# First projections of a diffusion step: order of the first loads, and modulation sums in column groups

## The chip, the cores and the metric

The program runs on one core of one Trainium2 chip. The metric is the time of one execution in device microseconds (us). TensorE is called PE here, VectorE DVE, ScalarE ACT, GpSimd POOL, and SyncE, which issues the transfers, SP.

## The reference

One layer of a backbone is computed for 128 context tokens and 2048 latent tokens of width 1024, all in float32. What matters here is the start of it:

```python
m = silu(cond) @ w_mod + b_mod          # cond: c_ctx and c; w_mod: 1024 x 6144
sh1, sc1, ga1, sh2, sc2, ga2 = split(m, 6)
h = rmsnorm(x, norm_mix) * (1 + sc1) + sh1
proj = h @ w_in                          # 1024 x 3088
q, k, v = split(silu(centred_conv(proj[:, :1536], conv_w)), 3)
```

So `h` needs the first 2048 columns of `m`, that is 8 MB of `w_mod`, and the first projections need `h` and the columns of `w_in` that make k. A gated DeltaNet scan, spatial gating, the output projection and the MLP follow, and the outputs are both token streams and the scan's final states.

## The kernel before

The kernel is written with a tile framework. A planner orders the instructions of every engine by a simulated timeline in which instructions that stand earlier in the program go first where several are ready; it also assigns buffers and waits. The order on an engine, SP's queue included, is fixed when the program is built; an engine whose next instruction waits does nothing else.

The 17 tiles of 128 tokens are projected in six blocks (`BLOCKS`), of which block 0 holds the context tile and two latent tiles. In a block, twelve feature tiles of 128 columns are projected: (1, h) are k, (0, h) q and (2, h) v. Every projection is float32-like: inputs and weights are split in a high and a low part (`split_w`, L200 on ACT and L201 on DVE), and three products (L226 to L228) per 128 rows of weights are accumulated. A feature tile thus has 8 x 3 products in one accumulator (`pj`, three buffers; `pt`, three buffers, for transposes and for the feature tile (1, 2) of block 0). Then it is evicted by the convolution (`convolve`: L553 on ACT, L556 on DVE).

Block 0's inputs need the modulation. `mod_load` loads half of one vector's weights, eight tiles of 128 x 512 (`raw`, L189), and `mod_sum` sums them in eight float32 products with `scond` (two columns, one per condition) as the weight (L337). ACT copies the row out (L339), `mod_out` turns it into columns with four transposes (L346) and adds the bias on DVE (L349, L353). `m0` and `r0` are the first half of the shift `b1`, `m1` and `r1` that of the scale `a1`, `m2` and `m3` the second halves. The first halves serve columns 0 to 3 of the inputs, the second ones columns 4 to 7.

`norm_rows` normalises a row tile (L320, L322). `column(k)` of block 0 transposes 128 columns of three row tiles (L499), applies scale and shift on ACT (L501), splits on DVE (L504, L505) into `kH` and `kL`, sets edge and halo columns on POOL (L491, L492; L494, L495), and stores both to DRAM (L519, four stores per column). `first_half` prepares the halo columns (L424 to L428). The next block's rows come with `load_x` (L447), whose squares ACT sums (L452); they use the three buffers of `xs0`.

Order of the loads on SP before: `m0`, the small vectors, `m1`, `m2`, the ten halo rows `xh`, three row tiles `xs0`, `m3`, four tiles of `W1[1]`, then the rest of `W1[1]` and `W1[0]` among column stores. `WARM` is 8: that many products of ones (L296) open the program on PE.

Of the kernel before, what the change touches and what calls it, by code (L numbers as in the profile page):

```python
# [8 lines left out]
F32 = mybir.dt.float32  # L9
# [8 lines left out]
P = 128  # L18
# [45 lines left out]
def hybrid_step(  # L64
# [11 lines left out]
    def xrow(t):  # L76
        return x_prompt[0] if t == 0 else x_sample[0, (t - 1) * P : t * P, :]
# [98 lines left out]
    def pm1():  # L176
        return pmp.tile([P, 512], F32, tag="pm", name="pm", bufs=2)
# [102 lines left out]
    with ExitStack() as ph:  # L280
# [52 lines left out]
        def mod_sum(raws, psum):  # L333

            pm = psum()
            for k in range(KT):
                T.matmul(pm[0:2, :], scond[:, k, :], raws[k], start=k == 0, stop=k == KT - 1)  # L337
            row = pf.tile([2, 512], F32, tag="first", name="first", bufs=2)
            A.copy(row, pm[0:2, :])  # L339
            return row  # L340

        def mod_out(row, half, dst, bias, scaled):

            pc = pm1()
            for i in range(4):
                T.transpose(pc[:, 2 * i : 2 * i + 2], row[:, i * P : (i + 1) * P], ident[0:2, 0:2])  # L346
            ks = slice(half * 4, half * 4 + 4)
# [8 lines left out]
        def split_mod_steps(jc):  # L356
# [23 lines left out]
            return [lambda k=k: f(k) for k in range(KT)]  # L380

        m0 = mod_load(0, 0)
# [12 lines left out]
        for m in range(5):  # L395
            load(out=xh[2 * m : 2 * m + 2, :], in_=x_sample[0, 255 + 384 * m : 257 + 384 * m, :])
        r2 = mod_sum(m2, pj)
# [7 lines left out]
        V.tensor_copy(hal, ps[:, 0:80].rearrange("p (k j) -> p k j", k=KT))  # L405
        xs0 = []
        for t in BLOCKS[0]:
            x = p1.tile([P, D], F32, tag="x", name="x", bufs=3)
            load(out=x, in_=xrow(t))
            xs0.append(x)  # L410
        for x in xs0:
            norm_rows(x)

        def load_w1(gi, ks):
            return [w1_raw(gi, k) for k in ks]

        def w1_raw(gi, k):
            return raw_w(w_in[0, k * P : (k + 1) * P, gi * 512 : (gi + 1) * 512])

# [10 lines left out]
        def prep_block(bi):  # L430
# [49 lines left out]
            if bi == 0:  # L480
                zc, hc = [0, 129, 130], [(387, 1)]
            elif bi == 5:
                zc, hc = [n + 1], [(0, 8)]
            else:
                hc = [(0, 2 * bi - 2), (n + 1, 2 * bi + 1)]
            def column(k):
                full = p1.tile([P, 384], F32, tag="full", name="full", bufs=2)
                kH = p1.tile([P, 388], F32R, tag="h", name="kH", bufs=24)
                kL = p1.tile([P, 388], F32R, tag="h", name="kL", bufs=24)
                for col in zc:  # L490
                    G.tensor_copy(kH[:, col : col + 1], zcol[:, 0:1])  # L491
                    G.tensor_copy(kL[:, col : col + 1], zcol[:, 0:1])  # L492
                for col, j in hc:
                    G.tensor_copy(kH[:, col : col + 1], f32(halH)[:, k, j : j + 1])  # L494
                    G.tensor_copy(kL[:, col : col + 1], f32(halL)[:, k, j : j + 1])  # L495
                if bi == 0:
# [32 lines left out]
        def feature_tile(blk, bi, gi, h):  # L529
# [229 lines left out]
        wr = load_w1(0, range(KT))  # L759
        us = [feature_tile(blk, 0, 1, h) for h in range(3)]  # L760
        for k in range(4):
            cols[k]()
            for u in us:
                u["main"][k]()
        mod_out(r3, 1, a1, vec[:, 8:16], True)
        W1[1] += [split_w(r) for r in wk]
        first_half(1)
# [1191 lines left out]
```

## Time and profile before

| | us |
|---|---|
| three runs | 2596.32, 2599.12, 2601.89 |
| median | 2599.12 |
| the profiled execution, its own time | 2598.87 |
| its span in the profile | 2596.8 |

In the profile, busy time is by engine, PE for products and PEld for the loading of their weights. L337 is line 337 of the kernel; an entry such as `pm<-raw,scond` names the tile written and the tiles read. "SPq" is SP's queue issuing a transfer. "idle before" gives the time that the engine stood idle ahead of an instruction, and who ended it. A float32 product is two records on PE. Records of products overlap, so the cost of a product is read from start to start.

### The profile page before, as it was taken

The numbers are of one execution on the slowest core, as the hardware profiler recorded it, in microseconds if no ns is written. First come the engines' busy times: TensorE is split into PE (matmuls) and PEld (weight loads), VectorE is DVE, ScalarE is ACT, GpSimd is POOL, SyncE is SP. The second block draws the span as 40 slices with busy tenths as digits, with TensorE's granted clock in tenths as the row PEclk, the third lists the DMA queues.
The fourth block names the chain that finished last, engine by engine and source line by source line (L and its number), as shares of the span: only waits on it lengthen the run. The fifth ranks groups of instructions, "written<-read, shape, count | busy, mean of one in ns | idle before, by whom it ended". The sixth has DMA issues, their size and how long they took to land.

```text
span 2596.8 us, 44648 instructions
## 1 busy us (share of the span) xinstructions
PE 2553.3 (98%) x15508; PEld 2156.5 (83%) x15508; DVE 1801.0 (69%) x3733; ACT 1220.9 (47%) x3048; POOL 228.8 (9%) x448
## 2 busy tenths in 40 slices
PE   9999999899999999999999999999999999999998
PEld 5999999688888787778888888888888888888887
DVE  5867756766667878886678876666665557784874
ACT  4755555554555667764355643332342432243441
POOL 3112212111111111210000000000000000000000
PEclk9999999899999999999999999999999999999999
DMA  8977738645445657885768789444479979786773
GB/s 288 304 212 214 209 109 266 201 148 154 154 144 166 208 173 248 275 275 181 279 204 256 224 283 307 114 118 118 123 234 370 334 268 321 270 256 213 236 247 106
DMA packets 494695, 571.88 MB, mean 220 GB/s; under 512 B 35124, under 2 KB 297564, under 8 KB 490886
## 3 DMA queue, kind: packets, MB, share of 16 engines
q1 hardware_dynamic: 494470, 569.04, 68.2%
q8 instruction: 122, 2.00, 0.3%
q14 instruction: 103, 0.84, 0.1%
HBM read 389.23 MB, written 179.67 MB: 219 GB/s over the span
## 4 chain that ended last, share of the span: by engine, by line
PE 87%; DVE 5%; DMA 4%; ACT 1%; issue 1%; POOL 0%; SPq 0%; DVEq 0%; POOLq 0%; ACTq 0%
PE f L226 16%; PE f L228 16%; PE f L227 16%; PE pj L226 7%; PE pj L228 7%; PE pj L227 7%; PE pd L995 5%; PE f L1599 2%; PE pm L226 1%; PE pm L227 1%; PE pm L228 1%; PE pt L610 1%; PE pt L569 1%; DMA QK<-qk_d 1%; PE pd L1076 1%
## 5 line engine op out<-in xcount | busy, mean ns | idle before, releaser
L226 PE MATMUL f<-hop,zH 128*128 128x512 f32 x960 | 373.4, 389 | 1.2 <-ACT zH L1485 1.2
L228 PE MATMUL f<-hop,zL 128*128 128x512 f32 x960 | 373.4, 389 | 0.4 <-DVE zL L1479 0.4
L227 PE MATMUL f<-hop,zH 128*128 128x512 f32 x960 | 373.3, 389 | 0.0
L226 PE MATMUL f<-hop,wH 128*128 128x512 f32 x896 | 355.2, 397 | 0.3 <-DMA hop<-hop_d 0.3
L227 PE MATMUL f<-hop,wH 128*128 128x512 f32 x896 | 349.1, 390 | 0.0
L228 PE MATMUL f<-hop,wL 128*128 128x512 f32 x896 | 347.9, 390 | 0.0
L1485 ACT CAST zH<-zraw 128x512 fp32r<-128x512 f32 x240 | 147.2, 620 | 300.6 <-DMA zraw<-s_d 98.0
L226 PEld LDWEIGHTS f<-hop,zH 128*128 128x128 f32 x960 | 180.2, 188 | 39.2 <-ACT zH L1485 1.6
L228 PEld LDWEIGHTS f<-hop,zL 128*128 128x128 f32 x960 | 180.2, 188 | 38.5 <-DVE zL L1479 1.3
L227 PEld LDWEIGHTS f<-hop,zH 128*128 128x128 f32 x960 | 180.2, 188 | 37.6 <-issue 0.2
L1479 DVE TENSOR_TENSOR zL<-zraw,zH 128x512 fp32r<-128x512 f32 x240 | 162.8, 687 | 65.5 <-ACT zH L1485 51.0
L228 PEld LDWEIGHTS f<-hop,wL 128*128 128x128 f32 x896 | 168.2, 188 | 35.3
L226 PEld LDWEIGHTS f<-hop,wH 128*128 128x128 f32 x896 | 168.5, 188 | 33.0 <-issue 0.7
L227 PEld LDWEIGHTS f<-hop,wH 128*128 128x128 f32 x896 | 168.5, 188 | 32.4
L226 PE MATMUL pj<-kH,wH 128*128 128x386 f32 (+2 forms) x568 | 191.2, 339 | 1.2 <-ACT junk L586 1.1
L228 PE MATMUL pj<-kH,wL 128*128 128x386 f32 (+2 forms) x568 | 190.4, 336 | 0.0
L227 PE MATMUL pj<-kL,wH 128*128 128x386 f32 (+2 forms) x568 | 190.1, 336 | 0.1
L183 POOL TENSOR_TENSOR r<-rsq,nhalf 128x1 f32<-128x1 f32 (+1 forms) x38 | 25.5, 670 | 1428.8 <-DVE rsq L182 1428.8
L556 DVE SCALAR_TENSOR_TENSOR cv<-pj,vec,cv 128x384 f32<-128x384 f32 (+2 forms) x164 | 87.0, 539 | 53.5 <-ACT cv L553 52.2
L226 PEld LDWEIGHTS pj<-kH,wH 128*128 128x128 f32 x568 | 107.6, 190 | 4.3 <-issue 2.3
L227 PEld LDWEIGHTS pj<-kL,wH 128*128 128x128 f32 x568 | 108.0, 190 | 1.1 <-POOL kL L495 0.4
L1485 ACT CAST wH<-s 128x512 fp32r<-128x512 f32 x96 | 59.4, 621 | 104.8 <-DVE s L1479 102.9
(398 smaller groups left out, 5705.5 us busy)
## 6 DMA issues: line engine op xcount, KB each, us to landing
zraw<-z_d SPq DMA_DIRECT2D x212, 256.0 KB
raw<-in_w_ff_dram SPq DMA_DIRECT2D x128, 256.0 KB
hop<-hop_d SPq DMA_DIRECT2D x28, 1024.0 KB
z_d<-c SPq DMA_DIRECT2D x96, 256.0 KB
zraw<-s_d SPq DMA_DIRECT2D x96, 256.0 KB
raw<-in_w_mod_dram SPq DMA_DIRECT2D x80, 256.0 KB
r<-in_w_ff_dram SPq DMA_DIRECT2D x80, 256.0 KB
s_d<-s SPq DMA_DIRECT2D x64, 256.0 KB
```

The costliest lines, as they stand in the source:

```text
L183: G.tensor_tensor(out=out, in0=t[:np_, :n], in1=nhalf[:np_, :n], op=ALU.pow)
L226: T.matmul(ps, lh, rh, start=first and i == 0, stop=False, skip_group_check=more)
L227: T.matmul(ps, lh, rl, start=False, stop=False, skip_group_check=more)
L228: T.matmul(ps, ll, rh, start=False, stop=last and i == n - 1, skip_group_check=more)
L556: V.scalar_tensor_tensor(out=cv[:, o : o + m], in0=ps[:, s + sh : s + sh + m], scalar=convw[:, w, j : j + 1], in1=cv[:, o : o + m], op0=AL ...
L569: T.transpose(pq[:, i * P : (i + 1) * P], u["x2"][:, i * P : (i + 1) * P], ident)
L610: T.matmul(ps[:, i * P : (i + 1) * P], kTt[:, i * P : (i + 1) * P], rhs[:, i * P : (i + 1) * P], start=True, stop=True)
L995: T.matmul(p[:, h, :], lhs[:, h, :], rhs[:, h, :], start=True, stop=True)
L1076: T.matmul(py[:, h], u["X"][:, h, :], pm[:, h], start=True, stop=True)
L1479: V.tensor_tensor(out=out, in0=a, in1=b, op=op)
L1485: A.copy(h, src)
L1599: T.matmul(ps[:, c : c + P], self.raw[m, kh][:, kp, :], x0[kh][:, kp, :], start=first and kp == 0, stop=last and kp == 3)
```

## The change

Loads: the three row tiles come behind `m0` and ahead of `m1`, then `m1`, the halo rows, four tiles of `W1[1]`, `m2`, `m3`, the other four tiles, then `W1[0]`. An added edge keeps the stores of columns 0 to 3 behind the last load of `W1[0]` on SP.

Sums: `scond` is widened to 32 columns with zeros (`sc32`). Product k goes to the column group k % 4 of PE and so to partitions 32 (k % 4) of the accumulator. The whole 128 x 512 accumulator is copied out, and `mod_out` turns it into columns with four float32 products by `sel`, which also adds the four groups. All four sums use `pm`; `mod_out` uses `pt`.

Order on PE: 16 products of ones stand behind the first sum. `r2` follows the products of column 1, `r3` those of column 3, both held there by edges. The rows are normalised ahead of `r1`'s sum.

Block 0's edge columns are zeroed at the start, its halo columns copied by ACT instead of POOL. The feature tile (1, 2) of block 0 now takes a `pj` buffer.

```diff
+        sc32 = p1.tile([P, KT, 32], F32, tag="sc32", name="sc32", bufs=1)
+        V.memset(sc32, 0.0)
+        V.tensor_copy(sc32[:, :, 0:2], scond)
+        sel = p1.tile([P, 2], F32, tag="sel", name="sel", bufs=1)
+        V.tensor_tensor(out=sel, in0=ident[:, 0:2], in1=ident[:, 32:34], op=ALU.add)
+        for g in (64, 96):
+            V.tensor_tensor(out=sel, in0=sel, in1=ident[:, g : g + 2], op=ALU.add)
...
             pm = psum()
             for k in range(KT):
-                T.matmul(pm[0:2, :], scond[:, k, :], raws[k], start=k == 0, stop=k == KT - 1)
-            row = pf.tile([2, 512], F32, tag="first", name="first", bufs=2)
-            A.copy(row, pm[0:2, :])
+                g = 32 * (k % 4)
+                T.matmul(pm[g : g + 32, :], sc32[:, k, :], raws[k], start=k < 4, stop=k >= 4)
+            row = pf.tile([P, 512], F32, tag="first", name="first", bufs=2)
+            A.copy(row, pm)
             return row
...
-            pc = pm1()
+            pc = pt()
             for i in range(4):
-                T.transpose(pc[:, 2 * i : 2 * i + 2], row[:, i * P : (i + 1) * P], ident[0:2, 0:2])
+                T.matmul(pc[:, 2 * i : 2 * i + 2], row[:, i * P : (i + 1) * P], sel, start=True, stop=True)
...
+        def here():
+            return len(tc.nc.cur_bb.bb.instructions)
+
+        def behind(before, start, engine):
+            for x in tc.nc.cur_bb.bb.instructions[start:]:
+                if x.engine == engine:
+                    tc.add_manual_dep(x, before.name, mybir.DependencyInfo(
+                        mybir.DependencyClass.NoSync, mybir.DependencyReason.DATA), reason="order")
+
+        edges = []
+        for k in range(KT):
+            pair = [p1.tile([P, 388], F32R, tag="h", name=n, bufs=24) for n in ("kH", "kL")]
+            for t in pair:
+                G.tensor_copy(t[:, 0:1], zcol[:, 0:1])
+                G.tensor_copy(t[:, 129:131], zcol[:, 0:2])
+            edges.append(pair)
         m0 = mod_load(0, 0)
         load(out=vec, in_=v_columns)
         convw = vec[:, 32:68].rearrange("p (w a) -> p w a", w=3)
+        xs0 = []
+        for t in BLOCKS[0]:
+            x = p1.tile([P, D], F32, tag="x", name="x", bufs=3)
+            load(out=x, in_=xrow(t))
+            xs0.append(x)
         m1 = mod_load(0, D)
-        r0 = mod_sum(m0, pm1)
-        r1 = mod_sum(m1, pj)
-        m2 = mod_load(1, 0)
-        mod_out(r0, 0, b1, vec[:, 0:8], False)
-
-        make_masks()
...
+        w1a = load_w1(1, range(4))
+        m2 = mod_load(1, 0)
+        m3 = mod_load(1, D)
+        w1b = load_w1(1, range(4, KT))
+        r0 = mod_sum(m0, pm1)
+        start = here()
+        for _ in range(2 * WARM):
+            T.matmul(warm[:, P : 2 * P], ones, ones, start=True, stop=True)
+        behind(tc.nc.cur_bb.bb.instructions[start - 2], start, mybir.EngineType.PE)
+        for x in xs0:
+            norm_rows(x)
         norm_rows(xh)
+        r1 = mod_sum(m1, pm1)
+        mod_out(r0, 0, b1, vec[:, 0:8], False)
+        make_masks()
...
                 for col, j in hc:
-                    G.tensor_copy(kH[:, col : col + 1], f32(halH)[:, k, j : j + 1])
-                    G.tensor_copy(kL[:, col : col + 1], f32(halL)[:, k, j : j + 1])
+                    for dst, src in ((kH, halH), (kL, halL)):
+                        if bi == 0:
+                            A.copy(dst[:, col : col + 1], f32(src)[:, k, j : j + 1])
+                        else:
+                            G.tensor_copy(dst[:, col : col + 1], f32(src)[:, k, j : j + 1])
...
-                    u["ps"] = (pt if bi == 0 and j == 6 else pj)()
+                    u["ps"] = pj()
...
-        m3 = mod_load(1, D)
-        wr = load_w1(1, range(4))
         mod_out(r1, 0, a1, vec[:, 8:16], True)
-        r3 = mod_sum(m3, pm1)
-        mod_out(r2, 1, b1, vec[:, 0:8], False)
-        W1[1] += [split_w(r) for r in wr]
+        W1[1] += [split_w(r) for r in w1a]
         first_half(0)
...
-        wk = load_w1(1, range(4, KT))
         wr = load_w1(0, range(KT))
+        last_load = tc.nc.cur_bb.bb.instructions[-1]
         us = [feature_tile(blk, 0, 1, h) for h in range(3)]
+        r2 = r3 = None
         for k in range(4):
+            start = here()
             cols[k]()
+            behind(last_load, start, mybir.EngineType.SP)
             for u in us:
                 u["main"][k]()
+            if k % 2:
+                start = here()
+                done = tc.nc.cur_bb.bb.instructions[-1]
+                if k == 1:
+                    r2 = mod_sum(m2, pm1)
+                else:
+                    r3 = mod_sum(m3, pm1)
+                behind(done, start, mybir.EngineType.PE)
+        mod_out(r2, 1, b1, vec[:, 0:8], False)
         mod_out(r3, 1, a1, vec[:, 8:16], True)
-        W1[1] += [split_w(r) for r in wk]
+        W1[1] += [split_w(r) for r in w1b]
```

More of the change, by code (lines that the diff above doesn't have):

```diff
@@ L380, in split_mod_steps, with load_w1, w1_raw @@
             return [lambda k=k: f(k) for k in range(KT)]
+        def load_w1(gi, ks):
+            return [w1_raw(gi, k) for k in ks]
+        def w1_raw(gi, k):
+            return raw_w(w_in[0, k * P : (k + 1) * P, gi * 512 : (gi + 1) * 512])
+        def here():
[12 more added lines that the diff above has]
+            edges.append(pair)
         m0 = mod_load(0, 0)
@@ L405, in hybrid_step @@
         V.tensor_copy(hal, ps[:, 0:80].rearrange("p (k j) -> p k j", k=KT))
[L406 to L418, printed above, removed]
         W1 = {0: [], 1: [], 2: []}
@@ L480, in prep_block @@
             if bi == 0:
-                zc, hc = [0, 129, 130], [(387, 1)]
+                zc, hc = [], [(387, 1)]
             elif bi == 5:
@@ L487, in column @@
                 full = p1.tile([P, 384], F32, tag="full", name="full", bufs=2)
-                kH = p1.tile([P, 388], F32R, tag="h", name="kH", bufs=24)
-                kL = p1.tile([P, 388], F32R, tag="h", name="kL", bufs=24)
+                if bi == 0:
+                    kH, kL = edges[k]
+                else:
+                    kH = p1.tile([P, 388], F32R, tag="h", name="kH", bufs=24)
+                    kL = p1.tile([P, 388], F32R, tag="h", name="kL", bufs=24)
                 for col in zc:
@@ L493, in column @@
                 for col, j in hc:
-                    G.tensor_copy(kH[:, col : col + 1], f32(halH)[:, k, j : j + 1])
-                    G.tensor_copy(kL[:, col : col + 1], f32(halL)[:, k, j : j + 1])
+                    for dst, src in ((kH, halH), (kL, halL)):
+                        if bi == 0:
+                            A.copy(dst[:, col : col + 1], f32(src)[:, k, j : j + 1])
+                        else:
+                            G.tensor_copy(dst[:, col : col + 1], f32(src)[:, k, j : j + 1])
                 if bi == 0:
@@ L757, in hybrid_step @@
         load(out=abr, in_=w_ab)
-        wk = load_w1(1, range(4, KT))
         wr = load_w1(0, range(KT))
+        last_load = tc.nc.cur_bb.bb.instructions[-1]
         us = [feature_tile(blk, 0, 1, h) for h in range(3)]
+        r2 = r3 = None
         for k in range(4):
+            start = here()
             cols[k]()
+            behind(last_load, start, mybir.EngineType.SP)
             for u in us:
                 u["main"][k]()
+            if k % 2:
[3 more added lines that the diff above has]
+                    r2 = mod_sum(m2, pm1)
+                else:
+                    r3 = mod_sum(m3, pm1)
+                behind(done, start, mybir.EngineType.PE)
+        mod_out(r2, 1, b1, vec[:, 0:8], False)
         mod_out(r3, 1, a1, vec[:, 8:16], True)
-        W1[1] += [split_w(r) for r in wk]
+        W1[1] += [split_w(r) for r in w1b]
         first_half(1)
```

1 line of the change is left out of this document (removed).

## The prediction

> **What bounds the kernel now.** I read the page's head and chain first, then busy time by stretch, then the start of the program instruction by instruction on PE, SP and ACT.
>
> ```profile
> span 2596.8 us, 44648 instructions
> PE 2553.3 (98%) x15508; PEld 2156.5 (83%) x15508; DVE 1801.0 (69%) x3733; ACT 1220.9 (47%) x3048; POOL 228.8 (9%) x448
> PE 87%; DVE 5%; DMA 4%; ACT 1%; issue 1%; POOL 0%; SPq 0%; DVEq 0%; POOLq 0%; ACTq 0%
> 5.00:36.00 31.00, 31.00 (x88) 6.81 (x87) 9.56 (x39) 8.78 (x16) 13.44 (x68) 1.00 0.99 354
> 36.00:60.00 24.00, 23.89 (x142) 22.87 (x142) 21.02 (x66) 16.54 (x36) 6.13 (x8) 1.00 0.79 247
> 60.00:80.00 20.00, 16.66 (x88) 15.59 (x87) 11.85 (x33) 13.56 (x44) 1.30 (x2) 0.91 0.96 315
> 130.00:380.00 250.00, 250.00 (x1597) 242.36 (x1596) 166.35 (x331) 138.04 (x425) 45.09 (x129) 1.00 0.64 188
> ```
>
> The window rows give length, then busy time and count for PE, PEld, DVE, ACT, POOL, then granted clock, DMA share and GB/s. PE sets the time, so a microsecond taken from PE's stream, or from a hole in it, comes off the end. Until 36 us PE and DMA are both full (0.99): what PE no longer does there counts only as far as the transfers let it. The one hole afterwards lies between 60 and 80 us:
>
> ```profile
> 68.37 0.34 PE L226 MATMUL pj<-kH,wH 128*128 128x388 f32 x1
> 70.37 0.52 PE L569 MATMUL pt<-ident,x 128*128 128x128 f32 x3 [1.66 <-DVE ab L641]
> 71.43 0.34 PE L228 MATMUL pj<-kH,wL 128*128 128x388 f32 x1
> 72.32 0.52 PE L569 MATMUL pt<-ident,x 128*128 128x128 f32 x3 [0.56 <-DVE x L560]
> 73.97 0.41 PE L226 MATMUL pj<-kH,wH 128*128 128x388 f32 x1 [1.13 <-ACT junk L586]
> 74.71 0.53 PE L226 MATMUL pj<-kH,wH 128*128 128x388 f32 x1
> 75.03 0.52 PE L227 MATMUL pj<-kL,wH 128*128 128x388 f32 x1
> 77.90 0.34 PE L227 MATMUL pj<-kL,wH 128*128 128x388 f32 x1
> 78.07 0.34 PE L228 MATMUL pj<-kH,wL 128*128 128x388 f32 x1
> ```
>
> A projection product costs 0.17 us from start to start (77.90 to 78.07). The hole is 1.8 us at 68.37, 0.7 at 71.43 and 1.4 at 72.32, by starts less the cost of the work between. From 74.71 to 75.03 the step is 0.32: for about eleven products the clock is half, another 1.6 us. In all some 5.5 us. Its cause is on ACT and SP:
>
> ```profile
> 56.82 1.35 ACT L553 ACTIVATE cv<-pj,vec 128x128 f32<-128x128 f32 x4 [3.77 <-PE pj L228]
> 59.40 0.53 ACT L559 ACTIVATE x<-cv 128x384 f32<-128x384 f32 x1 [1.23 <-DVE cv L556]
> 66.27 1.06 ACT L452 ACTIVATE junk<-x 128x1024 bf16<-128x1024 f32 x1 [6.35 <-DMA x<-in_x_sample_dram]
> 67.33 0.71 ACT L553 ACTIVATE cv<-pt,vec 128x128 f32<-128x128 f32 x2
> 38.31 6.97 SPq L189 DMA_DIRECT2D raw<-in_w_in_dram x12
> 45.62 0.33 SPq L519 DMA_DIRECT2D hH_d<-kH  x1
> 61.43 0.42 SPq L519 DMA_DIRECT2D hL_d<-kL  x1
> 61.94 0.44 SPq L447 DMA_DIRECT2D x<-in_x_sample_dram  x1
> ```
>
> ACT stands in its own order at the squares of block 1's first rows (L452) for 6.35 us; the eviction of the third feature tile (L553, 67.33) waits behind them. These rows are issued at 61.94, behind 28 column stores issued one after another from 45.62 on, 0.58 us each.
>
> **The change, part by part.** *Sums in column groups.* Four loads of eight weights, each product two records:
>
> ```profile
> 32.50 3.60 PE L337 MATMUL pm<-raw,scond 128*2 128x512 f32 x8
> 36.03 0.62 PE L226 MATMUL pj<-kH,wH 128*128 128x388 f32 x2
> 151.32 0.62 PE L265 MATMUL pm<-acc,pick 128*2 128x128 f32 x16
> 151.87 0.44 PE L226 MATMUL pj<-kH,wH 128*128 128x386 f32 x1
> ```
>
> Eight records take 3.53 us (32.50 to 36.03), 0.44 each, so 64 take 28.2. The kernel already has products in four column groups: L265, 16 records of 128 columns in 0.55 us, 0.034 each. Scaled to 512 columns that is 0.14, so 64 take 8.8 and 19.4 us of PE work go. Bounds: nothing goes (groups one after another), or three quarters, 21.2. I take the L265 row, the same form.
>
> *Added PE work.* 16 products of ones are 32 records of 128 columns, 0.11 each (0.44 / 4): 3.5 us, placed after the first sum, where PE would wait for rows and weights anyway. If that cover is missing they cost 3.5. Each of the four transposing steps (L346) becomes a float32 product of a full 128x128 weight: before 0.33 for four, now eight records of 0.11 to 0.24 (the last by L296, 3.78 / 16):
>
> ```profile
> 1.24 3.78 PE L296 MATMUL pt<-ones 128*128 128x128 f32 x16 [1.24 <-DVE ones L293]
> 38.47 0.41 PE L346 MATMUL pm<-ident,first 2*128 2x2 f32 x4
> 36.74 0.57 ACT L339 COPY first<-pm 2x512 f32<-2x512 f32 x1
> 39.66 0.23 DVE L353 SCALAR_TENSOR_TENSOR a<-a,vec 128x4 f32<-128x4 f32 x2
> 43.07 0.62 ACT L200 CAST wH<-raw 128x512 fp32r<-128x512 f32 x1
> 42.27 0.91 ACT L501 ACTIVATE full<-pt,b,a 128x128 f32<-128x128 f32 x2 [0.15 <-DVE kL L505]
> L494 POOL CAST kH<-halH 128x1 fp32r<-128x1 f32 x16 | 7.7, 511 | 10.1 <-DVE halH L427 8.6 <-DVE b L349 1.5
> ```
>
> That adds 0.6 to 1.6 us each; I take 1. The wider eviction is still 512 columns and keeps 0.57. The few DVE operations for `sc32` and `sel` lie before the first weights land; free.
>
> *Halo columns.* 32 copies leave POOL (L494, 511 ns each) and become ACT copies on block 0; ACT is busy 16.5 of 24 us there, so some 0.2 us each (an estimate: one column, where L339 takes 0.57 for 512) fit in. POOL's edge zeros are only named earlier. Zero on the path, at worst 1 us late per column.
>
> *Order of loads.* Bytes follow from the shapes (a weight tile is 0.262 MB, a row tile 0.524). Before, the transfers ran like this (last column GB/s):
>
> ```profile
> 0.00:18.50 18.50, 17.26 (x50) 6.32 (x51) 3.46 (x24) 2.07 (x3) 12.31 (x68) 1.00 0.90 313
> 0.00:23.00 23.00, 21.76 (x60) 7.17 (x61) 4.01 (x27) 3.35 (x5) 12.31 (x68) 1.00 0.88 305
> 0.00:34.50 34.50, 33.26 (x100) 10.18 (x101) 10.48 (x51) 9.12 (x16) 17.71 (x96) 1.00 0.92 325
> ```
>
> That is 5.8, 7.0 and 11.2 MB. In the new order the second modulation half-weight (`m1`) is complete after 5.8 MB, four projection weights after 6.9, `m3` after 11.1. So `m1` is there at 18.5 us, the weights at 23, `m3` at about 34.3. First projection: `m1` at 18.5, last sums 0.9, copy 0.57, products 1, additions 0.7, column 0.91 and about 1 on DVE, makes 24, against 36.03. Four columns at about 1.9 each (ACT: 0.91, 0.62 for the weight's split, two halo copies) are through at about 32; r2 waits for `m2` inside this and costs nothing more.
>
> *Second half.* Here the gain is cut: 34.3 for `m3`, sum 0.9, copy 0.57, products 1, additions 0.8, halo and column 2, makes 39.6. Before had then done 3.6 us of the work behind 36.03; after has done 36 products (6.3) and 12 transposes (about 1), 7.3. PE is thus ahead by some 4 us, less what it loses because the third tile now takes a `pj` buffer: three accumulators stand, and the fourth tile waits for the first convolution, some 1.3 us. Ahead: 2.8, bounds 0 and 5.
>
> *SP.* The stores of columns 0 to 3 are put behind the last load of `W1[0]`; behind them on SP stand the other stores and block 1's rows. The last load of `W1[0]` completes 14.3 MB: 34.3 plus 3.2 MB at 354 GB/s, 43.3; an issue leads its landing by about 4.3 (61.94 to 66.27), so SP is through with the loads at 39 to 41 (small ones between), against 45.28 now; but 32 stores follow instead of 28, and some small loads: 34 to 38 issues at 0.51 to 0.58. The rows are then issued at 56.5 to 62 (now 61.94); I take 59, 3 us earlier.
>
> *ACT's order* decides the rest. The planner now sees the three first tiles finished some 7 us earlier (near 50, against 56.82 for the first L553) and the rows only 3 earlier. Then the third tile's eviction goes ahead of the rows' squares, and ACT's wait falls where PE still has three tiles to project (72 products, 12.6 us). The 5.5 us hole goes; what is late next is the fourth tile's eviction, behind rows that land at about 63.3 (66.27 less 3).
>
> Sum: 2.8 + 5.5 = 8.3 us, less about 0.3 of new waits: 8. The profiled execution took 2598.87, 0.25 under the median of the three runs (2599.12); 2599.1 - 8 = 2591. From 130 us on PE is full to 380 and its chain goes on to the end, so I move that part rigidly.
>
> **The rivals.** *Rows still first on ACT.* If the planner leaves the squares ahead of the third tile's eviction, the chain of now stays: SP, rows, ACT, PE. The time follows the rows alone: 3 us gained (bounds 0 and 4.5), 2596. For it: the chain below runs exactly there today. Against: the tiles move further than the rows.
>
> ```profile
> 62.97 5.57 DMA x<-in_x_sample_dram
> 68.63 0.47 ACT junk L452
> ```
>
> *Slower: rows ahead of the first eviction.* Today the squares stand after two tiles' evictions. If they come ahead of the first one, no `pj` comes free until the rows are in: at 63.3, square 1.2, convolution 2.3, so PE begins the fourth tile at 67. It had finished six tiles when it restarted at 73.97; now three of those (12.6 us) still follow, 79.5 instead of 74. That is 5.5 slower, 2604.5. It decides once the squares precede the first L553 on ACT.
>
> *Groups don't overlap.* Each sum takes 7 us again; r2 and r3 then delay the second half to about 48, some 5 later than today's pace: 2604. L265 speaks against it.
>
> *The clock falls in the head.* Rows: after the hole at 68.37 to 73.97, about eleven products ran at 0.32 instead of 0.17. In the new head PE has little to do between 35 and 39.6 and may wait near 50; two such falls cost 3.2, so 2594. The Trainium skill, "TensorE: Matmul & The Clock Gate", section "HAM oscillation — how this bites in real kernels", says that idle gaps over about 3.4 us bring the clock back to half. The trace agrees after its one such stall; by that rule the gap near 35 would be slow each time, while the ones products guard only the earlier wait.
>
> **How the numbers follow.** Hole gone: 0.45, 2588 to 2594. Rows still first: 0.19, 2594.5 to 2599. Clock falls: 0.08, 2592 to 2596. Rows ahead of the first eviction: 0.18, 2602 to 2609 (the upper end if the rows are issued no earlier than now, 3 more, and the clock falls, 1.6). Groups one after another: 0.03, 2600 to 2606. Something that the planner orders differently further on: 0.07, either sign, 2 to 6 us. A measurement of this kernel tells about 0.2%, 5.2 us, from no change (three runs spread over 5.6). Faster than 2593.9: the first case, and a third each of the third and the last, 0.50. Slower than 2604.3: three quarters of the fourth case and half of the last two, 0.18. Within: 0.32. The range reaches from 2585, below the first case by the bound of the last, up to 2604, above which those 0.18 lie; the first case's own range is 2588 to 2594.
>
> **What would show it.** Right: L337 products of four groups starting together; first L226 near 24 us; a PE gap near 35 to 39; first L553 near 50; L447 issued near 59; L452 after the third L553 on ACT; PE with no hole between 60 and 75. Wrong: `m3` later than 35, L447 not before 61, a longer ACT wait for rows ahead of an L553, or half-rate products after 36.

## The result and the profile after

The changed kernel took 2606.13 us (median; 2604.98 to 2610.93), the kernel before 2597.92 beside it: a ratio of 1.0036, 95% interval 1.0025 to 1.0047. By the ratio it is 9.4 us slower, where 8 us faster had been forecast. The page's head, and busy time in the stretches that were shown of the kernel before (length, then busy time and count of PE, PEld, DVE, ACT, POOL, then granted clock, DMA share, GB/s):

```profile
span 2603.3 us, 44729 instructions
0.00:34.50 34.50, 29.33 (x132) 19.16 (x133) 14.44 (x62) 13.39 (x32) 16.83 (x72) 0.85 0.92 320
5.00:36.00 31.00, 27.04 (x130) 16.26 (x134) 13.57 (x50) 11.90 (x30) 12.55 (x44) 0.83 0.99 350
36.00:60.00 24.00, 20.60 (x130) 16.42 (x122) 15.76 (x47) 14.94 (x35) 0.00 (x0) 1.00 0.92 280
60.00:80.00 20.00, 16.17 (x85) 15.88 (x86) 13.74 (x35) 13.54 (x40) 1.10 (x1) 0.83 0.87 281
```

PE was full from 5 to 60 us before. Now it idles 4.0 us until 36 and 3.4 until 60, and the granted clock is 0.83 in the first of these stretches. From 60 to 80 us it again idles 3.8, though the old hole at 68 to 74 is gone. The projection's progress shows where the time goes: the count of L226 products that had started by a time, first before, then after (the first count in brackets; a few records can be missing, so a difference of one or two says nothing). The last line of each gives all of these products that were recorded, their least, median and longest time in ns, and the starts of the first and the last.

```profile
0.00:60.00 60.00, 9.37 (x32) 5.73 (x33) 1.00 0.87 295
0.00:100.00 100.00, 26.72 (x81) 15.67 (x82) 0.98 0.87 284
0.00:140.00 140.00, 45.72 (x136) 25.79 (x136) 0.99 0.87 281
L226 PE MATMUL pj<-kH,wH x568: 278/339/527, 36.0 to 427.5; 128*128 128x386 f32 x128, 128*128 128x258 f32 x32, 128*128 128x388 f32 x30
```

```profile
0.00:60.00 60.00, 7.66 (x24) 4.90 (x24) 0.91 0.92 306
0.00:100.00 100.00, 25.90 (x74) 15.06 (x75) 0.91 0.89 284
0.00:140.00 140.00, 41.06 (x119) 23.43 (x119) 0.93 0.89 279
L226 PE MATMUL pj<-kH,wH x576: 276/339/665, 29.8 to 438.3; 128*128 128x386 f32 x128, 128*128 128x388 f32 x32, 128*128 128x258 f32 x32
```

Each L226 stands for three products, 0.53 us of PE in the first blocks (3 x 0.175). After 60 us PE is 8 behind (4.2 us, and it stands still until 63.83), after 100 us 7, after 140 us 17 (9.0 us). The last of these products starts 10.8 us later (438.3 for 427.5), so little is lost between 140 us and there. The two profiled executions end only 6.5 us apart; why the rest is shorter in the second isn't shown. By the count, more than half of the lag is made between 100 and 140 us, where block 0 ends and block 1 begins. In that stretch, first before, then after, PE was full and now idles 3.3 us (40.00 less 36.71), 2.09 of them until 131.18, and the clock isn't full:

```profile
100.00:140.00 40.00, 39.97 (x249) 39.11 (x248) 31.25 (x65) 24.39 (x78) 9.96 (x36) 1.00 0.87 275
100.00:140.00 40.00, 36.71 (x223) 33.80 (x222) 28.98 (x58) 18.68 (x50) 11.72 (x32) 0.96 0.90 266
```

PE in the changed kernel, row by row (start, duration):

```profile
15.85 4.96 PE L346 MATMUL pm<-raw,sc 128*32 128x512 f32 x16
24.51 1.87 PE L355 MATMUL pt<-sel,first 128*128 128x2 f32 x8
29.79 1.31 PE L226 MATMUL pj<-kH,wH 128*128 128x388 f32 x3 [0.75 <-DVE halL L456]
35.09 1.92 PE L346 MATMUL pm<-raw,sc 128*32 128x512 f32 x16
40.32 1.93 PE L346 MATMUL pm<-raw,sc 128*32 128x512 f32 x16
44.38 1.05 PE L355 MATMUL pt<-sel,first 128*128 128x2 f32 x8
49.78 0.59 PE L226 MATMUL pj<-kH,wH 128*128 128x388 f32 x2 [1.14 <-ACT kH L527]
58.52 0.33 PE L228 MATMUL pj<-kH,wL 128*128 128x388 f32 x1
63.83 0.66 PE L226 MATMUL pj<-kH,wH 128*128 128x388 f32 x1 [4.98 <-DVE cv L590]
64.29 0.53 PE L227 MATMUL pj<-kL,wH 128*128 128x388 f32 x1
64.61 0.53 PE L228 MATMUL pj<-kH,wL 128*128 128x388 f32 x1
```

The first half begins at 29.79 (36.03 before), the second only at 49.78, and a new hole of 5.1 us follows at 58.5 (63.83 less 58.52 less 0.175). After it the step between products is 0.32 (64.29 to 64.61) in place of 0.175 for eleven of them, 1.6 us more. ACT's rows, and below them SP's, say why:

```profile
20.78 1.06 ACT L328 ACTIVATE junk<-xh 10x1024 bf16<-10x1024 f32 x1 [5.28 <-DMA xh<-in_x_sample_dram]
21.84 0.56 ACT L348 COPY first<-pm 128x512 f32<-128x512 f32 x1
43.22 0.62 ACT L200 CAST wH<-raw 128x512 fp32r<-128x512 f32 x1 [1.99 <-DMA raw<-in_w_in_dram]
43.75 0.58 ACT L348 COPY first<-pm 128x512 f32<-128x512 f32 x1
57.12 0.62 ACT L200 CAST wH<-raw 128x512 fp32r<-128x512 f32 x1 [4.57 <-DMA raw<-in_w_in_dram]
58.77 1.99 ACT L200 CAST wH<-raw 128x512 fp32r<-128x512 f32 x3 [1.02 <-DMA raw<-in_w_in_dram]
60.66 1.35 ACT L587 ACTIVATE cv<-pj,vec 128x128 f32<-128x128 f32 x4
63.18 1.06 ACT L480 ACTIVATE junk<-x 128x1024 bf16<-128x1024 f32 x1 [1.18 <-DMA x<-in_x_sample_dram]
```

```profile
43.23 0.33 SPq L553 DMA_DIRECT2D hH_d<-kH  x1
53.02 2.63 SPq L189 DMA_DIRECT2D raw<-in_w_in_dram  x4
56.22 1.07 SPq L475 DMA_DIRECT2D x<-in_x_sample_dram  x2
```

Three times ACT stands, in its fixed order, at work whose data are not in, with the urgent instruction right behind it: r1's row (21.84) behind the squares of the halo rows, r3's row (43.75) behind the split of a `W0` weight, the first eviction (60.66) behind four splits of v's weights. Those weights are issued at 53.02, behind sixteen stores that begin at 43.23.

### The profile page after: what moved, and what is told of

The parts are those of the page before. It is cut to its first block, busy times and chain, and to the rows that moved or that the text cites. A ratio compares the mean times of both kernels' runs of the same rounds, so it can differ in the third digit from the quotient of the medians.

```text
span 2603.3 us, 44729 instructions
## 1 busy us (share of the span) xinstructions
PE 2551.9 (98%) x15556; PEld 2163.9 (83%) x15556; DVE 1804.8 (69%) x3738; ACT 1220.2 (47%) x3064; POOL 228.5 (9%) x416
## 4 chain that ended last, share of the span: by engine, by line
PE 85%; DMA 6%; DVE 5%; ACT 2%; issue 1%; SPq 1%; POOL 0%; DVEq 0%; POOLq 0%; ACTq 0%
PE f L226 16%; PE f L228 16%; PE f L227 16%; PE pj L226 7%; PE pj L228 6%; PE pj L227 6%; PE pd L1037 4%; PE f L1641 2%; PE pm L226 1%; PE pm L227 1%; PE pm L228 1%; DMA raw<-in_w_mod_dram 1%; PE pt L644 1%; PE pt L603 1%; PE pd L1118 1%
## 5 line engine op out<-in xcount | busy, mean ns | idle before, releaser
L226 PE MATMUL f<-hop,zH 128*128 128x512 f32 x960 | 373.4, 389 | 1.2 <-ACT zH L1527 1.2
L226 PE MATMUL f<-hop,wH 128*128 128x512 f32 x896 | 355.3, 397 | 0.0
L226 PEld LDWEIGHTS f<-hop,zH 128*128 128x128 f32 x960 | 180.2, 188 | 39.2 <-ACT zH L1527 1.6
L226 PE MATMUL pj<-kH,wH 128*128 128x386 f32 (+2 forms) x576 | 194.3, 341 | 6.9 <-DVE cv L590 5.0
L226 PEld LDWEIGHTS f<-hop,wH 128*128 128x128 f32 x896 | 168.5, 188 | 32.7 <-issue 0.4
L226 PEld LDWEIGHTS pj<-kH,wH 128*128 128x128 f32 x576 | 109.8, 191 | 10.5 <-issue 8.3
L228 PEld LDWEIGHTS pj<-kH,wL 128*128 128x128 f32 x576 | 110.1, 191 | 0.5
```

What stands on the lines that cost most here:

```text
L226: T.matmul(ps, lh, rh, start=first and i == 0, stop=False, skip_group_check=more)
L228: T.matmul(ps, ll, rh, start=False, stop=last and i == n - 1, skip_group_check=more)
```

## The experiments

The theory after this profile: the gain of the earlier first half is real, and is lost in these three waits. It leaves out what is lost after 100 us. The rivals: the sums in groups cost more than they save; transfers set the pace whatever the order; or the loss lies in later blocks. Medians stand beside those of the kernel before on the same chip (2596.3 to 2598.2), and ratios are to it. Edits are to the changed kernel unless the kernel before is named; c9 is short for c9_pt_xh_pst.

**The parts of the change.** First the column groups alone, put into the kernel before.

```diff
-                T.matmul(pm[0:2, :], scond[:, k, :], raws[k], start=k == 0, stop=k == KT - 1)
...
+                T.matmul(pm[g : g + 32, :], sc32[:, k, :], raws[k], start=k < 4, stop=k >= 4)
...
-                T.transpose(pc[:, 2 * i : 2 * i + 2], row[:, i * P : (i + 1) * P], ident[0:2, 0:2])
+                T.matmul(pc[:, 2 * i : 2 * i + 2], row[:, i * P : (i + 1) * P], sel, start=True, stop=True)
```

> The kernel before with the sums in column groups alone (loads, order and buffers as before, no added products of ones). The sums fall from 28 to about 9 us of PE. If the first weights' landing sets the pace, the first projection comes 2 to 4 us earlier and the time falls by 0 to 4 us, the stall at 68 us staying. If PE's sums were the bound, it falls by 8 or more. If the groups do not overlap, the time does not move or grows by 2.

2602.09, ratio 1.0014 (1.0004 to 1.0023). PE in this kernel:

```profile
37.72 0.42 PE L226 MATMUL pj<-kH,wH 128*128 128x388 f32 x1 [0.56 <-ACT wH L200]
53.47 1.01 PE L226 MATMUL pj<-kH,wH 128*128 128x388 f32 x2 [3.60 <-POOL kH L503]
```

The sums cost some 20 us less on PE (four of 1.85 for 28.2), and the first projection comes at 37.72, later than the 36.03 of before. PE now waits for modulation weights (1.45 us, until 28.57) and for ACT's split of a weight. So in the old order of loads the sums lay under the transfers, and taking them away doesn't bring the first projection forward. The 0.14% at the end are not the sums' alone: the kernel also waits 3.60 us for halo columns, which POOL copies here, and half clock follows. The other way round, the changed kernel with its groups undone, `scond` of two columns and the transposes back:

```diff
-                T.matmul(pm[g : g + 32, :], sc32[:, k, :], raws[k], start=k < 4, stop=k >= 4)
+                T.matmul(pm[0:2, :], scond[:, k, :], raws[k], start=k == 0, stop=k == KT - 1)
...
-                T.matmul(pc[:, 2 * i : 2 * i + 2], row[:, i * P : (i + 1) * P], sel, start=True, stop=True)
+                T.transpose(pc[:, 2 * i : 2 * i + 2], row[:, i * P : (i + 1) * P], ident[0:2, 0:2])
```

> The changed kernel with the column groups undone: sums in eight products of one group each, four transposes per row again; order of loads, edges and buffers as changed. If the head is bound by landings and by the orders on ACT and PE, the first sum still lies under the transfers, but r2 and r3 now stand in PE's order between columns at 7 us each in place of 1.85: product 54 comes some 5 to 8 us later than in the changed kernel, 2611 to 2615. Rival, that PE's work in the head counts for nothing: 2605 to 2608.

2611.62, ratio 1.0061 (1.0048 to 1.0075).

```profile
33.17 7.03 PE L337 MATMUL pm<-raw,scond 128*2 128x512 f32 x16
```

Here r2 and r3 stand in PE's order between columns and cost 7.03 us each, against 1.85 in groups; the loss against the changed kernel is 0.25%, some 6.5 us. So the groups do what they should, and help where a sum stands in PE's way. That they cost the changed kernel more than they save is ruled out.

**The three waits, one at a time.** The third feature tile back in `pt`, so that the fourth has a free accumulator:

```diff
-                    u["ps"] = pj()
+                    u["ps"] = (pt if bi == 0 and j == 6 else pj)()
```

> The changed kernel with one part undone: the feature tile (1, 2) of block 0 takes a pt buffer again, so that four feature tiles can stand. Accumulators theory (the stall of 5.3 us at 58.5 and the half clock after it, 1.7 us, come from the third pj buffer): PE has the fourth tile's 24 products (4.2 us) to do there, the stall falls under 1.5 us, no half-rate products follow, and the time falls by 5 to 7 us against the changed kernel, to about the kernel before. Rival, a later wait takes its place (rows, stores, loads queued on SP): the stall at 58.5 goes but PE stands as long elsewhere before 140 us, and the time falls by less than 2.

2602.25, ratio 1.0017 (1.0007 to 1.0026). The fourth tile's products now go ahead of the hole, but it stays: PE waits 3.88 us until 65.27 for the convolution on DVE. By the ratio 0.19%, 4.9 us, came back. So the time is near the first reading and the hole is as the rival had it. The splits of v's weights put behind the second eviction on ACT:

```diff
+                    u["ev"] = tc.nc.cur_bb.bb.instructions[-1]
...
+        def v_weight(k):
+            start = here()
+            W1[2].append(load_split(w_in[0, k * P : (k + 1) * P, 1024:1536]))
+            behind(us[1]["ev"], start, mybir.EngineType.Activation)
```

> The changed kernel, with the splits of the v weights held behind the second feature tile's eviction on ACT; three pj buffers as in the changed kernel. If ACT's order (four splits that wait for loads, ahead of the first eviction) makes the stall at 58.5, the first eviction starts near 57.5 instead of 60.7, the stall falls from 5.3 to about 2, the clock does not fall, and the time falls by 4 to 6 us. If the count of accumulators alone makes it, the stall stays above 4.

2607.11, ratio 1.0039 (1.0027 to 1.0050). The wait at 58.4 falls to 2.44 us and its half clock goes, but PE waits again ahead of 74.29 (1.39) and of 114.26 (2.18). The time of the changed kernel stays: an order on ACT alone moves the wait. The squares of the halo rows put behind r1's copy, and r1's columns ahead of the halo transposes on PE:

```diff
-        norm_rows(xh)
         r1 = mod_sum(m1, pm1)
+        r1_copy = tc.nc.cur_bb.bb.instructions[-1]
         mod_out(r0, 0, b1, vec[:, 0:8], False)
+        mod_out(r1, 0, a1, vec[:, 8:16], True)
...
+        start = here()
+        norm_rows(xh)
+        behind(r1_copy, start, mybir.EngineType.Activation)
...
+        behind(last, start, mybir.EngineType.PE)
```

> The changed kernel, with the square of the ten halo rows held behind the copy of r1 on ACT, their transposes behind the columns of r1 on PE, and the columns of r1 made at once. If the late first projection (29.8 instead of the 24 forecast) comes from the halo rows standing ahead of r1, the first projection starts near 25 to 26, r3 is summed near 36 to 37 instead of 40.3, and the second half begins some 3 to 4 us earlier; the time falls by 3 to 4. If the second half hangs on the loads, only the start moves and the time stays within 1.5 us.

2601.57, ratio 1.0017 (1.0006 to 1.0028). ACT and PE in this kernel:

```profile
20.71 0.58 ACT L348 COPY first<-pm 128x512 f32<-128x512 f32 x1 [5.21 <-PE pm L346]
37.49 3.45 ACT L200 CAST wH<-raw 128x512 fp32r<-128x512 f32 x5 [2.59 <-DMA raw<-in_w_in_dram]
59.01 0.42 PE L226 MATMUL pj<-kH,wH 128*128 128x388 f32 x1 [1.84 <-DVE cv L597]
```

The row is copied at 20.71 (21.84), and the first projection comes at 27.97 (29.79). r3's sum ends at 39.3, but its copy stands behind splits that wait for loads until 40.84. About half of the loss is gone, as the first reading had it, but not for its reason: the second half begins at 49.00, only 0.8 us earlier than in the changed kernel. What went is most of the hole. In this kernel's order the first eviction (56.32) stands ahead of the splits of v's weights, PE waits 1.84 us in place of 4.98, and its clock stays full there. So this edit also took away most of the third wait. Next the splits of `W0` held behind the scale and shift of columns 4 to 7 on ACT:

```diff
+        last_col = [x for x in tc.nc.cur_bb.bb.instructions if x.engine == mybir.EngineType.Activation][-1]
...
+        def q_weight(r):
+            start = here()
+            W1[0].append(split_w(r))
+            behind(last_col, start, mybir.EngineType.Activation)
```

> The changed kernel with the splits of W0 held on ACT behind the last scale-and-shift of columns 4 to 7. If the second half is late because ACT stands at W0 splits that wait for loads, r3's row is copied at 42.3 in place of 43.75 and the second half begins at 47 to 48 in place of 49.8; the eight splits then stand ahead of the first eviction, so that the hole at 58.5 stays at 5 us or grows: 2604 to 2607. If it is late because r3's sum itself is (behind column 3's products and m3's landing), it begins at 49 or later, and the time is 2606 or more.

2610.28, ratio 1.0057 (1.0044 to 1.0070). ACT and PE in this kernel:

```profile
42.79 0.58 ACT L348 COPY first<-pm 128x512 f32<-128x512 f32 x1 [1.20 <-PE pm L346]
48.30 0.59 PE L226 MATMUL pj<-kH,wH 128*128 128x388 f32 x2
70.33 1.06 ACT L480 ACTIVATE junk<-x 128x1024 bf16<-128x1024 f32 x1 [8.16 <-DMA x<-in_x_sample_dram]
```

The copy now waits for the sum alone, and the second half begins at 48.30, 1.5 us earlier: from the sum's end at 42.5 it needs some 6 us by its own chain (copy, columns, DVE, scale and shift, halo). Then ACT stands 8.16 us at block 1's rows with evictions behind them. The start lies between the two readings, and the time fits the second alone. The second wait, taken away by itself, gives nothing: the order of an engine isn't mended at one place.

**SP's queue.** Block 0's stores issued by POOL's queue, nothing else:

```diff
-                        store(out=by_tiles(dst[:, :, k, :], at),
+                        (nc.gpsimd.dma_start if bi == 0 else store)(
+                              out=by_tiles(dst[:, :, k, :], at),
```

> The changed kernel with block 0's 32 column stores issued by POOL's queue in place of SP's. If SP's queue, in which v's weights are issued behind 16 stores (53.0) and rows behind 32, sets the hole at 58.5, both are issued some 8 to 16 us earlier, and the time is 2597 to 2601. If transfers are full (DMA 0.87 to 0.96 busy from 36 to 60), the loads land no earlier by much and the hole keeps most of its 5 us: 2603 to 2607.

2603.84, ratio 1.0018 (1.0009 to 1.0027).

```profile
46.32 2.86 SPq L189 DMA_DIRECT2D raw<-in_w_in_dram  x4
63.64 0.41 PE L226 MATMUL pj<-kH,wH 128*128 128x388 f32 x1 [1.84 <-DVE cv L591]
```

v's weights are issued 6.7 us and the rows (51.15) 5.1 us earlier, and the hole of 5 us becomes one of 1.84 without half clock behind it. The second half begins later, though (51.74, at half clock): stores now go beside the loads of `W0`, the likely cause, and ACT waits longer for these. By the ratio some 4.7 us of the loss is SP's queue.

**Together.** Tile in `pt` and halo squares late (as in e1_pt and e5_xh):

> The changed kernel with the third tile back in pt, and the halo rows' squares behind r1's copy. Alone the two took 3.9 and 4.5 us. If they act on two separate waits (three accumulators full at 58.5; r1's row late at 22), they add: 2597 to 2599, about the kernel before. If both only bring PE earlier to the same wait for the first eviction, 2600 to 2602.

2601.13, ratio 1.0015 (1.0005 to 1.0024), hardly better than either alone. The splits of v's weights stand ahead of the first eviction again, and PE waits 2.92 us for it, until 66.27. With `W0`'s splits late as well (as in e10_wqlate):

> The kernel of the run before with the splits of W0 also held behind the last scale-and-shift of columns 4 to 7. If ACT's weight splits set when the second half begins, it begins at 46 to 47 and the time is 2594 to 2597; if the first eviction, now behind eight more splits, sets the pace, 2599 to 2602.

2607.01, ratio 1.0040 (1.0026 to 1.0054). PE and SP in this kernel:

```profile
78.36 0.87 PE L610 MATMUL pt<-ident,x 128*128 128x128 f32 x3 [8.68 <-DVE cv L597]
68.73 1.41 SPq L482 DMA_DIRECT2D x<-in_x_sample_dram  x3
```

PE had as many L226 by 60 us as the kernel before (32), and then stands 8.68 us: the rows are issued only at 68.73, behind all the stores. The third set takes the stores off SP in place of moving the splits:

> The changed kernel with the third tile in pt, the halo squares behind r1 and block 0's stores on POOL's queue. Alone they took 3.9, 4.5 and 4.7 us off. If they are three waits of their own, 2593 to 2596; if all three shorten the same wait (first eviction at 58.5 to 63.8, behind splits that wait for the weights of v), 2598 to 2602.

2597.79, ratio 1.0003 (0.9994 to 1.0012): level with the kernel before. Alone the three edits gave 0.19%, 0.19% and 0.18% back, together 0.33%, 8.6 of the 9.4 us. So these three parts of the change make up most of the loss. They don't add, and how the loss divides among the waits isn't shown. This version wins nothing over the kernel before either, although its first half starts 8.8 us earlier (27.21). PE in this kernel:

```profile
53.80 0.90 PE L540 MATMUL pt<-ident,x 128*128 128x128 f32 x3 [1.42 <-ACT full L542]
54.36 1.00 PE L226 MATMUL pj<-kH,wH 128*128 128x388 f32 x2
```

The second half begins at 54.36, later than in the changed kernel: ACT's scale and shift stands behind splits of `W0`, which wait for their loads. So the start of the second half doesn't set the time. It came at 48.30 in e10_wqlate, the slowest of these. What does go with the time, roughly, is how long PE idles from 56 to 140 us: 1.1 us in c9 (ratio 1.0003), 3.3 in a_pst, 4.7 in e5_xh and 6.5 in e1_pt (1.0017 to 1.0018), 8.3 in the changed kernel (1.0036), 8.6 in e3_wv (1.0039) and 12.1 in e10_wqlate (1.0057), from one profile of each.

**What the old hole was worth.** The forecast gave 5.5 us to the hole at 68 to 74 us of the kernel before. Here its supposed cause is moved in that kernel alone: the squares of block 1's rows stand behind four evictions. The edit moves a second thing, in its last lines: the rest of block 1's preparation, the factors of its rows and the loads of its columns, comes one feature tile later.

```diff
+                if bi == 1:
+                    rows1.append(x)
+                else:
+                    square(x, t)
...
+                    start = here()
+                    for x, t in zip(rows1, tiles):
+                        square(x, t)
+                    behind(evicted[3], start, mybir.EngineType.Activation)
...
-                    side += nxt[1][n : n + 1]
+                    m = n - (bi == 0 and n > 3)
+                    side += nxt[1][m : m + 1] if (bi, n) != (0, 3) else []
```

> The kernel before with one thing moved: ACT's squares of block 1's rows stand behind the evictions of the first four feature tiles, in place of ahead of the third. If the hole at 68 to 74 us is ACT standing at rows that are not in, as the forecast had it, its 5.5 us go and stay gone: 2591 to 2593. If PE then only reaches earlier a wait that other loads (weights of v, modulation weights) set, the hole comes back later and smaller: 2594 to 2597.

2601.33, ratio 1.0017 (1.0008 to 1.0027): slower. ACT and PE at the hole, and the count of L226 by 100 and by 140 us:

```profile
68.94 0.62 ACT L200 CAST wH<-raw 128x512 fp32r<-128x512 f32 x1 [5.50 <-DMA raw<-in_w_in_dram]
72.66 0.41 PE L226 MATMUL pj<-kH,wH 128*128 128x388 f32 x1 [2.45 <-DVE ab L665]
0.00:100.00 100.00, 28.34 (x87) 16.17 (x88) 1.00 0.84 275
0.00:140.00 140.00, 45.00 (x135) 25.11 (x135) 1.00 0.88 281
```

The hole shrinks and doesn't close. ACT no longer stands at rows, but 5.50 us at a split of a projection weight that isn't in, and PE waits 2.45 us in place of 1.66, 0.56 and 1.13, at full clock. So the rows were not all of the hole's cause. At 100 us the kernel is six products ahead of the kernel before (87 to 81, 3.2 us), at 140 us one behind (135 to 136). So what was won there doesn't come off the end: between 100 and 140 us the kernel before does 55, this one 48, and PE idles 2.1 us there where it idled none. The changed kernel does 45 there, e5_xh 48, c9_pt_xh_pst 50. That the later preparation takes the lead back wasn't tested. Two other causes were tried. Transfers (DMA 1.06 busy from 100 to 130 us in the kernel before), by moving four modulation steps with their loads out of that stretch, in b_sq, in the kernel before, and in c9:

```diff
-MOD_STEPS = (1, 1, 0, 0, 0, 1, 0, 2, 0, 1, 1, 2)
+MOD_STEPS = (1, 1, 0, 0, 0, 1, 0, 2, 0, 0, 0, 0)
```

> The run b_sq with four steps of the later modulation sums, with one load of 256 KB each, moved out of block 0's last three feature tiles into later blocks. If transfers bind the stretch of 100 to 130 us, PE keeps most of the 4 us that it had won at 94 us: 2594 to 2597. If the waits there come from the order on ACT and DVE, whatever is loaded, 2599 to 2602 as b_sq.

> The kernel before with the same four steps moved alone. PE has no hole from 80 us on there, so nothing is to be won: 2596 to 2600 by either theory; it is slower only if the four steps cost more where they now stand.

> The run c9_pt_xh_pst with the four modulation steps moved out of block 0's end as well. If full transfers from 100 to 130 us take back what PE is ahead by at 90 us, this is 2 to 4 us faster than c9_pt_xh_pst; if not, the same.

2600.47 (1.0012, 1.0003 to 1.0021), 2599.05 (1.0005, 0.9996 to 1.0015) and 2601.15 (1.0016, 1.0007 to 1.0024). Nothing is kept, and c8 is no better than c9. And ACT's waits for the next rows, by moving the squares in every block:

> The kernel before with the squares of the next block's rows behind three evictions in every block, not only in block 0. If ACT's waits for the rows of block 2 (2.84 and 1.10 us in b_sq) take back what the closed hole gives, 2594 to 2597. If every engine's order there has waits enough to take it back, 2599 to 2602, as b_sq.

> The run c9_pt_xh_pst (2597.8, level with the kernel before) with the squares of rows moved as in b_sqall. If rows on ACT are what is left, 2592 to 2595, the only version faster than the kernel before; if not, 2597 to 2600.

2600.31 (1.0015, 1.0006 to 1.0023) and 2599.04 (1.0012, 1.0002 to 1.0021). Neither is the cause alone. The squares late in the two combined kernels as well:

> The run c4_pt_xh (2601; hole of 3.3 us at 63 where the first row of block 1 is late) with the squares of block 1 behind the first four evictions. If rows are what ACT stands at, the hole goes: 2597 to 2599. If weight splits that wait for loads stand there too, 2600 to 2602.

> The changed kernel with the third tile in pt, halo squares behind r1, W0's splits behind columns 4 to 7 (the run c6_pt_xh_wql, 2607, where ACT stood 9.0 us at the first row of block 1 and PE 8.8 from 69.3 on), and the squares of block 1 behind the first four evictions. If this wait, and not work, made the time, PE reaches product 156 some 7 us earlier than the kernel before (c6_pt_xh_wql had it 0.7 earlier at product 132, and the kernel before stands 5.5 us there): 2591 to 2596 in the end. If the wait goes on to the weights of v or the transposes for tokens: 2598 to 2602.

2602.60 (1.0015, 1.0006 to 1.0024) and 2610.48 (1.0043, 1.0029 to 1.0057): no gain, and in the second PE still stands 8 us at 70. Both have the later preparation too, as have the other runs with moved squares. What takes back the lead between 100 and 140 us stays open. No version was faster than the kernel before.

## Why the prediction was wrong, step by step

The sum had two terms, 2.8 us of lead at the second half and 5.5 us for the hole. The first failed at the path from landing to use, which was reckoned as if ACT and PE were free: the second half began at 49.78 and not at 39.6, so there was no lead, and the wait for the fourth tile, put at 1.3 us, took 5.1 and half clock behind it. The second failed in that the hole's 5.5 us were carried to the end: the old hole went, a new one came, and b_sq kept nothing of the 3.2 us that it won at the old one. Step by step:

- *Sums in groups*: right. 16 records in 1.85 us (35.09 to 36.94) against 7.03; 8.8 for four had been reckoned, 7.4 follows. `mod_out` by products takes 0.95 to 1.05, as reckoned, except r1's, on the way to the first projection, which took 1.87 (24.51) at half clock.
- *Landings*: the changed kernel moved 11.0 MB by 34.5 us (320 GB/s), so by bytes `m3`, complete after 11.1, lands where it was put. The step from landing to use failed.
- *First projection at 24*: 29.79. The sum listed `m1`'s chain as if nothing stood before it on ACT and PE. Of the 5.8 us, 1.4 are the sum's, which ends at 20.8 and not 19.4, and 1.0 the copy's: ACT stood 5.28 us for the halo rows, and r1's copy came behind their squares. Another 2.9 are r1's columns, which end at 26.4 (24.51 and 1.87) where the forecast's terms give 21.0: PE did the halo transposes ahead of them and ran at half clock. e5_xh takes 1.8 of the 5.8 us away.
- *Second half at 39.6*: 49.78, the largest miss, 10.2 us. Of these 7.0 are the sum's: it ends at 42.2 in place of 35.2, since an edge holds it behind column 3's products, and these start 5.8 later, with r2's 1.85 ahead of them ("costs nothing more" was wrong, it stands in line). 1.5 go to the copy's wait behind the split at 43.22, and 1.7 to a longer chain from the copy on.
- *Fourth tile, "some 1.3 us"*: 5.1, and 1.6 of half clock. The three first tiles are projected side by side and end together at 58.5, so no accumulator is free until a first eviction and its convolution are through: 3.2 us, from 60.66 to 63.83. Splits of v's weights took the rest. The prediction looked on ACT for rows ahead of evictions, and not for weights.
- *SP*: the rows at 56.2 (59 forecast, 56.5 to 62 as range), the stores from 43.2 (39 to 41). That the rows came near is luck: the first two stand behind 16 stores and the loads of v's weights, and not behind 32 stores. v's weights, which stand behind the same 16 stores, were not traced at all.
- *ACT's order*: wrong. Two squares (63.18 and the next) still go ahead of the third eviction, as in the first rival; they no longer wait long (1.18 us for 6.35), since the rows come earlier and the evictions later.
- *"Hole gone" gives 5.5 at the end*: the old hole went in the changed kernel, and a new one came at 58.5. Its cause was taken to be rows alone; in b_sq weights kept ACT waiting in their place. And the 3.2 us won there were gone by 140 us. The rule that a hole ahead of a full stretch comes off the end failed: the stretch behind it isn't rigid, and PE idles in it where it was full.
- *The slower rival* named the right mechanism, no `pj` free behind a wait on ACT, but with the wrong load ahead of the eviction: weights of v and not rows. It priced the whole at 5.5 us slower; 9.4 were measured.
- *The clock*: two falls were feared, three came: half clock from 23.4 to 33.6, from 60.9 to 67.7 and from 132.6 to 136.0 us. The first slows r1's columns by some 0.8 us and the products around 32 by as much, the second costs 1.6. The prediction read the stall at 68.37 to 73.97 as one gap; its rows show three waits of 1.66, 0.56 and 1.13 us with work between them, so that trace didn't bear out the bound that the prediction cites.

## What to carry to other kernels

An in-order engine makes a late load a wait for everything behind it; when loads are re-ordered, list for each engine what stands ahead of each urgent instruction, and when the data of each of those land, the weights of a later stage too. PE work that lies under a full transfer stage can be worth nothing (20 us less of it did not bring the first projection forward in e2_groups), but the same saving counts where it stands in line (e9_serial). And in a kernel whose engines are ordered by a planner, a closed hole is not a gain before the stretch behind it has been seen to keep it.

## What the runs showed of the hardware

PE's clock fell to half with single waits of 2 to 3 us. In the changed kernel a wait of 2.75 us (20.8 to 23.55) goes with the first fall and one of 2.09 (129.09 to 131.18) with the third; both stretches of half clock as windows:

```profile
23.40:33.60 10.20, 9.25 (x39) 8.25 (x40) 7.59 (x30) 5.83 (x19) 8.42 (x26) 0.50 1.02 369
132.60:136.00 3.40, 3.40 (x22) 2.78 (x24) 3.36 (x7) 1.07 (x2) 0.00 (x0) 0.50 1.07 368
```

In c4_pt_xh it fell after a wait of 2.92 us:

```profile
66.27 0.42 PE L226 MATMUL pj<-kH,wH 128*128 128x388 f32 x1 [2.92 <-DVE cv L597]
66.90:70.30 3.40, 3.40 (x12) 3.40 (x11) 2.84 (x8) 1.88 (x5) 0.00 (x0) 0.50 0.75 194
```

The clock doesn't fall at once: the products at 66.53 and 66.71 still ran at full clock, 0.18 us apart. A wait of 2.45 us in b_sq (72.66, above) left the clock full, so the length of the wait alone doesn't decide. The Trainium skill, "TensorE: Matmul & The Clock Gate", section "HAM oscillation — how this bites in real kernels", sets the bound at gaps over about 3.4 us. The falls after 3.60 us in e2_groups and 4.98 in the changed kernel agree with it; those after 2.09, 2.75 and 2.92 us don't, nor does the one in the kernel before, after three waits of 1.66, 0.56 and 1.13 us.

A float32 product in four column groups runs 3.8 times as fast as one after another (16 records in 1.85 against 7.03 us).
